# Weight tiles 32 bytes longer: the high and low parts of split weights start at other addresses

## The chip, the cores and the metric

The kernel runs on one core of a Trainium2 chip. The metric is the device time of one execution in microseconds. The engines named here are TensorE (PE; its weight loads are listed apart as PEld), VectorE (DVE), ScalarE (ACT), GpSimd (POOL) and SyncE (SP, which issues DMAs).

## The reference

One encoder layer on 512 tokens with 1,024 features, in float32. `x` passes three residual blocks, each behind an RMS norm with a shift and scale computed from a conditioning vector `c`:

```
x += 1/2 * g1 * SwiGLU_1(mod(RMSNorm(x)))
x += g2 * W_out( sig(gA) * W_A(WindowGQA+sink) + sig(gB) * W_B(DiffAttn) )
x += 1/2 * g3 * SwiGLU_2(mod(RMSNorm(x)))
```

The two SwiGLU blocks have an inner width of 2,816; `w_mod` (1,024 x 9,216) gives the nine modulation vectors. Between the blocks lie a windowed attention with 8 heads and a differential attention with 4 heads.

## The kernel before

All activations are kept feature-major: a tile holds 128 features and up to 512 tokens. To keep float32 accuracy on a faster matmul type, each operand is split into a high part (the value rounded to that type) and a low part (the rest), and a product is made of three matmuls: high weight by high activation, high weight by low activation, low weight by high activation. `mm3` (lines 153 to 156) does this with 512 or 256 tokens a matmul. In the second feed-forward block a Strassen-like scheme of seven products is used instead, and its helper `two` (lines 1098 to 1100) issues the same three matmuls with 256 tokens. In both, the weights are the stationary operand, which TensorE loads ahead of each matmul, and the activations the moving one. In `project` (lines 656 to 658) it is the other way round: activations are stationary and the weight tiles move through.

A weight block of 128 x 1,024 comes by DMA into a `raw` tile. `split_from` (lines 159 and 160) then writes the high part into a `hi` tile on ScalarE and the low part into a `lo` tile on VectorE. Four places allocate such a pair: `load_split` (first feed-forward, mixing, gates), `first_split` (the first eight blocks), `load_main` (projections and gates; there the low part is made by ScalarE and a DMA that adds), and `Unit.prepare` (second feed-forward). `hi` and `lo` have five buffers each, used in turn; the k-th pair of a stage has the same buffer number in both. Some weights go elsewhere: three gate blocks are split into `u4` tiles (`load_split(..., spare=True)`), and one block of the second feed-forward into a `b8` tile.

The order of the matmuls on TensorE is fixed by the program: written out by hand at the boundaries of the blocks, and by a list of items in the second feed-forward block. Weights are asked for some items ahead.

All tiles lie in one pool. It gives every kind of tile one stretch of each partition's memory, in order of first use, its buffers one behind the other, each size rounded up to 32 bytes. From the sizes in the kernel before, the starts in a partition are:

| kind | buffers x bytes | first start | start counted by 128 | by 512 |
|---|---|---|---|---|
| `u4` (gate weights, some activations) | 6 x 4,096 | 6,048 | 32 | 416 |
| `x` (residual) | 8 x 2,048 | 31,040 | 64 | 320 |
| `ka` | 1 x 4,096 | 47,712 | 96 | 96 |
| `b8` (split activations) | 12 x 8,192 | 51,808 | 96 | 96 |
| `f2` (scratch) | 8 x 2,048 | 150,112 | 96 | 96 |
| `raw` | 4 x 4,096 | 166,496 | 96 | 96 |
| `hi` | 5 x 4,096 | 182,880 | 96 | 96 |
| `lo` | 5 x 4,096 | 203,360 | 96 | 96 |

Inside a tile, weights begin at multiples of 512 bytes and activations at multiples of 1,024 (512 or 256 tokens), so every such operand of `ka`, `b8`, `hi` and `lo` begins at 96 by 512, and every one of `u4` at 416. [...]

Of the kernel before, what the change touches and what calls it, by code (L numbers as in the profile page):

```python
# [12 lines left out]
F32R = mybir.dt.float32r  # L13
# [5 lines left out]
P = 128  # L19
# [78 lines left out]
RAW, HILO, LO, F2 = 4, 5, 5, 8  # L98
# [16 lines left out]
def layer(ctx: ExitStack, tc: tile.TileContext, a: dict):  # L115
# [6 lines left out]
    def name(tag):  # L122
        count[0] += 1
        return f"{tag}_{count[0]}"

    def sbuf(tag, shape, dt, bufs):
        return sb.tile(shape, dt, name=name(tag), tag=tag, bufs=bufs)
# [4 lines left out]
    def f2():  # L132
        return sbuf("f2", [P, T], F32, F2)

    def b8(dt=F32R):
        return sbuf("b8", [P, 4, T], dt, 12)

    def u4(dt=F32R):
        return sbuf("u4", [P, 2, T], dt, 6)
# [4 lines left out]
    def bank(tag):  # L144
        return psum.tile([P, T], F32, name=name(tag), tag=tag, bufs={"acc": 3, "op": 1, "sc": 3, "tp": 1}[tag])
# [12 lines left out]
    def split_from(hi, lo, src):  # L158
        S.copy(hi, src)  # L159
        V.tensor_tensor(lo, src, f(hi), ALU.subtract)  # L160

    def load_split(src, n=1024, spare=False):
        raw = sbuf("raw", [P, 1024], F32, RAW)
        if spare:
            hi, lo = (u4().rearrange("p a b -> p (a b)") for _ in range(2))
        else:
            hi = sbuf("hi", [P, 1024], F32R, HILO)
            lo = sbuf("lo", [P, 1024], F32R, LO)
        nc.sync.dma_start(raw[:, 0:n], src)
        split_from(hi[:, 0:n], lo[:, 0:n], raw[:, 0:n])  # L170
        return hi, lo
# [22 lines left out]
    def mod_load(v, c):  # L194
        w = u4(F32).rearrange("p a b -> p (a b)")
        nc.sync.dma_start(w, a["w_mod"][v * NC + c])
        return w

    def mod_col(v, c, w=None, on_pool=False):
        if w is None:  # L200
            w = mod_load(v, c)
        t = modv[v][:, c : c + 1]
        if on_pool:
            S.activation(w, w, AF.Identity, accum_out=t)
        else:
            V.tensor_tensor_reduce(  # L206
                out=w, in0=w, in1=cact, scale=1.0, scalar=0.0, op0=ALU.mult, op1=ALU.add, accum_out=t
            )
        i = v * NC + c
        b = par[:, BMOD + i : BMOD + i + 1]  # L210
        if v in (SC1, SC2, SC3):
            n = {SC1: NORM1, SC2: NORM2, SC3: NORM3}[v]
            V.tensor_scalar(t, t, b, 1.0, ALU.add, ALU.add)
            V.tensor_tensor(t, t, par[:, n + c : n + c + 1], ALU.mult)
        elif v in (SH1, SH2, SH3):
            V.tensor_tensor(t, t, b, ALU.add)
        else:

            V.tensor_scalar(t, t, b, -0.5 if v == G3 and c % 4 < 2 else 0.5, ALU.add, ALU.mult)
# [62 lines left out]
    def hidden(rb, c, sc, sh, hi, lo, r=FULL[0]):  # L282

        t = f2()[:, r]
        s = modv[sh][:, c : c + 1]
        V.scalar_tensor_tensor(t, x[c][:, r], modv[sc][:, c : c + 1], rb, ALU.mult, ALU.mult)
        S.activation(hi[:, r], t, AF.Identity, bias=s)
        yield
        V.scalar_tensor_tensor(lo[:, r], t, s, f(hi[:, r]), ALU.add, ALU.subtract)
        yield  # L290
# [75 lines left out]
    def pair_banks():  # L366
        return (bank("acc"), bank("sc"))

    def ffn(w_in, w_out, g, hh, hl, begin, p, side, after_x, norm, loaded=None):
# [17 lines left out]
        for hf in range(2):  # L387
            while p < (hf + 1) * NH:
                u = loaded or [load_split(w_in[p, k]) for k in range(2)]
                loaded = None  # L390
                out = pair_banks()
                for k in range(NC):
                    ffn_pair_mm(u, k, out, hh, hl)
                finish(p, out)
                side(SIDE_IN)
                p += 1
# [34 lines left out]
    with tc.manual_schedule(engines={mybir.EngineType.DVE, mybir.EngineType.Activation, mybir.EngineType.PE}):  # L431
        cb = [bank("sc") for i in range(2)]
        for i in range(2):
            PE.matmul(cb[i], ones[0:1, :], crow[:, i * T : (i + 1) * T], start=True, stop=True)
        n1 = Norm()
        for c in range(NC):
            sq = f2()
            S.activation(sq, x[c], AF.Square)
            if c:
                V.tensor_tensor(sq, sq, before, ALU.add)  # L440
            before = sq
        n1.sums(sq, FULL[0], True, True)
        for i in range(2):
            S.activation(cact[:, i * T : (i + 1) * T], cb[i], AF.Silu)
        w1 = {}

        def first_loads(k):
            w1[k] = [mod_load(v, k) for v in ((SH1, SC1) if k else (SC1, SH1))]
            raw = sbuf("raw", [P, 1024], F32, RAW)
            nc.sync.dma_start(raw[:, 0:768], a["w1s"][k])  # L450
            w1[k].append(raw)
            if k:
                G.tensor_tensor(w1[k][0], w1[k][0], cact, ALU.mult)
                mod_col(SC1, k, w1[k][1])

        def first_split(k):
            hi = sbuf("hi", [P, 1024], F32R, HILO)
            lo = sbuf("lo", [P, 1024], F32R, LO)
            split_from(hi[:, 0:768], lo[:, 0:768], w1[k][2][:, 0:768])
            w1[k] = hi, lo  # L460

        first_loads(0)
        mod_col(SC1, 0, w1[0][0])
        rb1 = n1.spread(n1.diagonal(n1.rstd(FULL[0])))
        mod_col(SH1, 0, w1[0][1])
        first_split(0)
        out1 = [b for _ in range(3) for b in pair_banks()]
        for k in range(NC):
            h1 = hidden(rb1, k, SC1, SH1, hh[k], hl[k])
            next(h1)  # L470
            if k == 0:
                next(h1)
                first_loads(1)
            else:
                if k + 1 < NC:
                    first_loads(k + 1)
                next(h1)
            wh, wl = w1[k]
            for w, h in ((wh, hh[k]), (wl, hh[k]), (wh, hl[k])):
                for i, out in enumerate(out1):  # L480
                    last = k == NC - 1 and h is hl[k]
                    PE.matmul(out, w[:, i * P : (i + 1) * P], h, start=k == 0 and w is wh and h is hh[k], stop=last)
            if k + 1 < NC:
                mod_col(SH1, k + 1, w1[k + 1][0], on_pool=True)
                first_split(k + 1)
# [109 lines left out]
    def load_main(src):  # L595

        raw = sbuf("raw", [P, 1024], F32, RAW)
        nc.sync.dma_start(raw, src)
        hi = sbuf("hi", [P, 1024], F32R, HILO)
        lo = sbuf("lo", [P, 1024], F32R, LO)  # L600
        S.copy(hi, raw)
        S.activation(lo, raw, AF.Identity, scale=-1.0)
        G.dma_start(lo, src, accum_op=ALU.add)
        return hi, lo
# [12 lines left out]
    def first_gates(r):  # L617
# [13 lines left out]
    vb_w = boundary(  # L631
        last1, G1, n2, SC2, SH2, hh, hl, first_gates,
        lambda: [(load_split, load_main)[j // 2](a["w_vb"][j]) for j in range(4)],
        TO_MIX,
    )
# [28 lines left out]
    def gates(more=lambda: True):  # L664
        while gate_next[0] < 16 and more():
            j = gate_next[0]
            gate_next[0] += 1
            wh, wl = load_main(a["w_gate"][j])
            out = bank("acc")
            for k in range(NC):  # L670
                o = k * P
                mm3(out, wh[:, o : o + P], wl[:, o : o + P], hh[k], hl[k], k == 0, k == NC - 1)
                yield MM3
            gate_end(j, out)
# [427 lines left out]
    class Unit:  # L1102
# [25 lines left out]
        def prepare(self, q):  # L1128

            if q in self.ready:  # L1130
                return
            self.ask(q)
            n = self.depth * 2 * P
            if q in self.apart:
                both = b8().rearrange("p a b -> p (a b)")
                hi, lo = both[:, 0:n], both[:, 1024 : 1024 + n]
            else:
                hi = sbuf("hi", [P, 1024], F32R, HILO)[:, 0:n]
                lo = sbuf("lo", [P, 1024], F32R, LO)[:, 0:n]
            t = self.at[q]  # L1140
            split_from(hi, lo, t)
            self.ready[q] = hi, lo
            if q in self.more:
                s, src = self.more[q]
                G.dma_start(t, self.srcs[src], accum_op=ALU.add)
                self.at[s] = t
# [406 lines left out]
```

## Time and profile before

| | us |
|---|---|
| median of 3 runs | 1116.93 |
| lowest, highest | 1116.50, 1118.64 |
| the profiled execution | 1117.23 |
| its span, first to last instruction | 1115.4 |

| engine | busy us | share of span |
|---|---|---|
| TensorE, matmuls | 1086.0 | 97% |
| TensorE, weight loads | 950.5 | 85% |
| VectorE | 739.6 | 66% |
| ScalarE | 536.0 | 48% |
| GpSimd | 147.4 | 13% |

The views used below: the busy time of each engine in stretches of the span (the number behind x counts the instructions that begin there); the list of who waited for whom; groups of instructions by line with their shapes kept apart (count, then busy time and mean ns of one, then the idle time before them); and the instructions in order of time (start, length, engine, line, output <- inputs). Names of tiles are shortened there: `b` is `b8`, `u` is `u4`, `sc`, `acc`, `op` and `tp` are accumulators. Matmuls overlap, since one begins while the one ahead still drains, so the step from start to start, not the length, is what a matmul costs in a row of them.

### The profile page before, as it was taken

How to read it: one execution, taken by the hardware profiler on the slowest of the kernel's cores; microseconds unless marked ns; L12 is line 12 of the kernel's file. 1: busy time of each engine (PE TensorE's matmuls, PEld its weight loads, DVE VectorE, ACT ScalarE, POOL GpSimd, SP SyncE). 2: the span in 40 equal slices, each digit the busy share in tenths (PEclk: the TensorE clock that was granted, in tenths of full speed). 3: DMA queues.
4: the chain of work that ended last, by engine and by line, in shares of the span. 5: the costliest groups of instructions: out<-in, count | busy, mean ns of one | idle time of the engine just before them, and what ended most of it. 6: DMA issues, size and time to landing. Idle time of an engine off the chain costs nothing.

```text
span 1115.4 us, 16981 instructions
## 1 busy us (share of the span) xinstructions
PE 1086.0 (97%) x6540; PEld 950.5 (85%) x6540; DVE 739.6 (66%) x1441; ACT 536.0 (48%) x895; POOL 147.4 (13%) x152
## 2 busy tenths in 40 slices
PE   4899999999999999999999999999999999999998
PEld 2688888888888998876788877979999999999998
DVE  6998456765733450567642678855888777776767
ACT  3453221223223274567765655534766545654553
POOL 3300000000000011430113300101121111111210
PEclk9999999999999999999999999999999999999999
DMA  8797446766434439874468831862488999799874
GB/s 304 239 353 249 137 153 218 249 242 224 156 87 127 161 115 271 189 171 95 105 158 199 228 103 34 308 187 58 95 200 202 222 231 195 182 224 212 188 145 118
DMA packets 63570, 204.54 MB, mean 183 GB/s; under 512 B 7553, under 2 KB 9729, under 8 KB 63490
## 3 DMA queue, kind: packets, MB, share of 16 engines
q1 hardware_dynamic: 45792, 144.73, 37.6%
q0 software_dynamic: 15392, 54.53, 27.1%
q10 hardware_dynamic: 2306, 4.20, 1.0%
q8 instruction: 51, 0.84, 0.3%
q14 instruction: 29, 0.24, 0.1%
HBM read 194.52 MB, written 8.91 MB: 182 GB/s over the span
## 4 chain that ended last, share of the span: by engine, by line
PE 78%; issue 9%; DVE 5%; DMA 3%; ACT 2%; POOL 1%; SPq 0%; DVEq 0%; POOLq 0%; ACTq 0%
PE sc L154 9%; PE sc L156 9%; PE sc L155 9%; PE acc L154 7%; PE acc L155 6%; PE acc L156 6%; PE sc L1098 3%; PE sc L1100 3%; PE sc L1099 3%; PE acc L1099 3%; PE acc L1100 3%; PE acc L1098 3%; PE acc L656 2%; PE acc L657 2%; PE acc L658 2%
## 5 line engine op out<-in xcount | busy, mean ns | idle before, releaser
L159 ACT CAST hi<-raw 128x1024 fp32r<-128x1024 f32 (+2 forms) x160 | 155.3, 975 | 218.5 <-PE sc L155 130.9
L160 DVE TENSOR_TENSOR lo<-raw,hi 128x1024 fp32r<-128x1024 f32 (+2 forms) x160 | 179.9, 1129 | 60.6 <-ACT hi L159 58.4
L154 PE MATMUL sc<-b,hi 128*128 128x512 f32 (+1 forms) x430 | 159.9, 372 | 0.4 <-ACT b L159 0.4
L155 PE MATMUL sc<-b,hi 128*128 128x512 f32 (+1 forms) x430 | 159.3, 371 | 0.0
L156 PE MATMUL sc<-b,lo 128*128 128x512 f32 (+1 forms) x430 | 159.2, 370 | 0.0
L154 PE MATMUL acc<-b,hi 128*128 128x512 f32 (+1 forms) x352 | 134.1, 381 | 0.0
L155 PE MATMUL acc<-b,hi 128*128 128x512 f32 (+1 forms) x352 | 130.8, 372 | 0.0
L156 PE MATMUL acc<-b,lo 128*128 128x512 f32 (+1 forms) x352 | 130.7, 371 | 0.0
L1098 PE MATMUL acc<-b,hi 128*128 128x256 f32 x374 | 106.2, 284 | 0.1
L1099 PE MATMUL acc<-b,hi 128*128 128x256 f32 x374 | 105.9, 283 | 0.1
L1100 PE MATMUL acc<-b,lo 128*128 128x256 f32 x374 | 105.9, 283 | 0.0
L1100 PE MATMUL sc<-b,lo 128*128 128x256 f32 x358 | 101.4, 283 | 0.0
L1098 PE MATMUL sc<-b,hi 128*128 128x256 f32 x358 | 101.3, 283 | 0.0
L1099 PE MATMUL sc<-b,hi 128*128 128x256 f32 x358 | 101.3, 283 | 0.0
L154 PEld LDWEIGHTS sc<-b,hi 128*128 128x128 f32 x430 | 81.0, 188 | 14.7 <-ACT b L159 0.9
L155 PEld LDWEIGHTS sc<-b,hi 128*128 128x128 f32 x430 | 81.0, 188 | 14.2 <-DVE b L160 0.3
L156 PEld LDWEIGHTS sc<-b,lo 128*128 128x128 f32 x430 | 81.0, 188 | 13.7
L206 DVE CUSTOM_DVE_ANT_0 u<-u,ka 128x1024 f32<-128x1024 f32 x65 | 82.5, 1281 | 12.9 <-DMA u<-w_mod 12.8
L159 ACT CAST hi<-u 128x1024 fp32r<-128x1024 f32 (+1 forms) x51 | 52.2, 1024 | 69.1 <-PE acc L1099 14.1
L160 DVE TENSOR_TENSOR lo<-u,hi 128x1024 fp32r<-128x1024 f32 (+1 forms) x51 | 60.8, 1192 | 28.8 <-ACT hi L159 28.4
L154 PEld LDWEIGHTS acc<-b,hi 128*128 128x128 f32 x352 | 66.4, 189 | 13.7 <-issue 3.5
L156 PEld LDWEIGHTS acc<-b,lo 128*128 128x128 f32 x352 | 66.3, 188 | 11.3
(339 smaller groups left out, 2461.1 us busy)
## 6 DMA issues: line engine op xcount, KB each, us to landing
u<-w_mod SPq DMA_DIRECT2D x72, 512.0 KB, 5.3
raw<-w1i SPq DMA_DIRECT2D x38, 512.0 KB, 4.3
u<-w2i POOLq DMA_DIRECT2D x31, 512.0 KB, 6.1
raw<-w2i SPq DMA_DIRECT2D x31, 512.0 KB, 4.4
raw<-w_gate SPq DMA_DIRECT2D x16, 512.0 KB, 5.1
lo<-w_gate POOLq DMA_DIRECT2D x13, 512.0 KB, 7.3
u<-w2i SPq DMA_DIRECT2D x13, 512.0 KB, 6.9
raw<-w1o SPq DMA_DIRECT2D x16, 384.0 KB, 3.1
```

The lines of the kernel that those rows point to most:

```text
L154: PE.matmul(out, wh, xh, start=first, stop=False)
L155: PE.matmul(out, wh, xl, start=False, stop=False)
L156: PE.matmul(out, wl, xh, start=False, stop=last)
L159: S.copy(hi, src)
L160: V.tensor_tensor(lo, src, f(hi), ALU.subtract)
L206: V.tensor_tensor_reduce(out=w, in0=w, in1=cact, scale=1.0, scalar=0.0, op0=ALU.mult, op1=ALU.add, accum_out=t)
L656: PE.matmul(out[t][:, 0:n], hh[k][:, ht], wh[:, o : o + n], start=k == 0, stop=False)
L657: PE.matmul(out[t][:, 0:n], hh[k][:, ht], wl[:, o : o + n], start=False, stop=False)
L658: PE.matmul(out[t][:, 0:n], hl[k][:, ht], wh[:, o : o + n], start=False, stop=k == NC - 1)
L1098: PE.matmul(out, wh[:, s], xh, start=first and j == 0, stop=False, skip_group_check=True)
L1099: PE.matmul(out, wh[:, s], xl, start=False, stop=False, skip_group_check=True)
L1100: PE.matmul(out, wl[:, s], xh, start=False, stop=last and j == 1, skip_group_check=True)
```

## The change

The tiles `hi` and `lo` are declared with 1,032 in place of 1,024 columns, in all four places, and their first 1,024 columns are used as before. [...] `lo` begins 160 bytes further than before, and the tables behind it 320 bytes. No instruction, wait, transfer or order is added or taken away.

```diff
@@ load_split
-            hi = sbuf("hi", [P, 1024], F32R, HILO)
-            lo = sbuf("lo", [P, 1024], F32R, LO)
+            hi = sbuf("hi", [P, 1032], F32R, HILO)[:, 0:1024]
+            lo = sbuf("lo", [P, 1032], F32R, LO)[:, 0:1024]
@@ first_split
-            hi = sbuf("hi", [P, 1024], F32R, HILO)
-            lo = sbuf("lo", [P, 1024], F32R, LO)
+            hi = sbuf("hi", [P, 1032], F32R, HILO)[:, 0:1024]
+            lo = sbuf("lo", [P, 1032], F32R, LO)[:, 0:1024]
@@ load_main
-        hi = sbuf("hi", [P, 1024], F32R, HILO)
-        lo = sbuf("lo", [P, 1024], F32R, LO)
+        hi = sbuf("hi", [P, 1032], F32R, HILO)[:, 0:1024]
+        lo = sbuf("lo", [P, 1032], F32R, LO)[:, 0:1024]
@@ Unit.prepare
-                hi = sbuf("hi", [P, 1024], F32R, HILO)[:, 0:n]
-                lo = sbuf("lo", [P, 1024], F32R, LO)[:, 0:n]
+                hi = sbuf("hi", [P, 1032], F32R, HILO)[:, 0:n]
+                lo = sbuf("lo", [P, 1032], F32R, LO)[:, 0:n]
```

## The prediction

> **What bounds the kernel now.** I read the page's head and first part, then the busy time by stage, then TensorE's waits, and last, in order of time, the single matmuls, since the change moves addresses and nothing else. The page's first lines:
>
> ```profile
> span 1115.4 us, 16981 instructions
> PE 1086.0 (97%) x6540; PEld 950.5 (85%) x6540; DVE 739.6 (66%) x1441; ACT 536.0 (48%) x895; POOL 147.4 (13%) x152
> ```
>
> TensorE is busy 97% of the span. The sums below are made against this execution's own time, 1117.23 us (span 1115.4 and 1.8 around it); the median of the runs is 1116.93, so they differ by 0.03%. Three stretches of 56 us, with busy time and (x instructions) of PE, PEld, DVE, ACT and POOL, then the granted clock, the DMA share and GB/s:
>
> ```profile
> 56.00:112.00 56.00, 56.00 (x248) 46.16 (x247) 50.55 (x95) 23.14 (x32) 0.00 (x0) 1.00 0.83 300
> 840.00:896.00 56.00, 56.00 (x469) 56.00 (x469) 43.97 (x68) 32.70 (x52) 9.60 (x11) 1.00 0.88 212
> 896.00:952.00 56.00, 56.00 (x469) 56.00 (x469) 41.71 (x61) 30.05 (x43) 9.62 (x11) 1.00 0.93 215
> ```
>
> In the first feed-forward stage (56 to 112 us) TensorE takes 248 matmuls of 512 columns, 226 ns each; in the second (840 to 952 us) 469 of 256 columns, 119.4 ns each, and there the weight loads (PEld) fill all 56.00 us too. The clock is 1.00 in all three. TensorE's waits on a split are small; the longest in the list of waits (us in total, times, longest):
>
> ```profile
> PE acc L1100 <- DVE b L160: 0.8, 1, 0.8
> ```
>
> So TensorE's own step from matmul to matmul sets the time, and a weight tile's address can matter only through that step. Does it? The single matmuls (start, length, line) where the stationary operand goes over from a `hi`/`lo` buffer to a `u4` tile, while the moving operand stays in `b8`:
>
> ```profile
> 392.00 0.28 PE L154 MATMUL sc<-b,hi 128*128 128x256 f32 x1
> ...
> 392.96 0.28 PE L156 MATMUL sc<-b,lo 128*128 128x256 f32 x1
> 393.08 0.28 PE L154 MATMUL acc<-b,u 128*128 128x256 f32 x1
> 393.19 0.28 PE L155 MATMUL acc<-b,u 128*128 128x256 f32 x1
> ...
> 395.08 0.28 PE L156 MATMUL acc<-b,u 128*128 128x256 f32 x1
> ...
> 396.33 0.28 PE L156 MATMUL acc<-b,u 128*128 128x256 f32 x1
> ...
> 398.03 0.28 PE L156 MATMUL acc<-b,u 128*128 128x256 f32 x1
> ```
>
> From 392.00 to 393.08 there are nine steps with weights in `hi`/`lo`: 120.0 ns each. From 393.08 to 395.08 there are seventeen with weights in `u4`: 117.6 ns. After an interruption by eight short matmuls the same tiles go on at a third speed: fifteen steps from 396.33 to 398.03, 113.3 ns. The form, the clock and the moving tiles are the same. What differs between the first two is the start: `hi`, `lo` and `b8` begin at the same place in any 512 bytes, `u4` 64 bytes away from them by 128 (320 by 512). The same is seen where the moving operand goes to `u4` for six matmuls and the weights stay in `hi`/`lo`:
>
> ```profile
> 884.09 0.28 PE L1098 MATMUL acc<-u,hi 128*128 128x256 f32 x1
> ...
> 884.80 0.29 PE L1098 MATMUL op<-b,hi 128*128 128x256 f32 x1
> 884.93 0.28 PE L1099 MATMUL op<-b,hi 128*128 128x256 f32 x1
> ...
> 885.28 0.28 PE L1099 MATMUL op<-b,hi 128*128 128x256 f32 x1
> ```
>
> Six steps take 0.71 us, where 117.6 ns each would make 0.706 and 120.0 would make 0.72; then four steps back on `b8` take 0.48, the first of them 0.13. So a step of 256 columns depends on where the two operands begin relative to each other, and equal starts, the state of nearly all of this kernel, are the slow one of the two offsets seen.
>
> [...]
>
> **The change part by part.** (1) *New starts of the weights.* With 4,128 bytes a buffer, the five `hi` buffers begin 0, 32, 64, 96, 128 bytes further, and `lo`, behind them, 160 to 288 further. Counted by 128, against the moving `b8` tiles: `hi` 0, 32, 64, 96, 0; `lo` 32, 64, 96, 0, 32. Of three loads (hi, hi, lo) that makes (2 x 3/5 + 4/5) / 3 = 2/3 with a start that differs from the moving one. How many matmuls that is:
>
> ```profile
> L1098 PE MATMUL acc<-b,hi 128*128 128x256 f32 x374 | 106.2, 284 | 0.1
> L1098 PE MATMUL sc<-b,hi 128*128 128x256 f32 x358 | 101.3, 283 | 0.0
> L1098 PE MATMUL tp<-b,hi 128*128 128x256 f32 x66 | 18.7, 283 | 0.0
> L1098 PE MATMUL op<-b,hi 128*128 128x256 f32 x58 | 16.4, 283 | 0.0
> L154 PE MATMUL sc<-b,hi 128*128 128x256 f32 x76 | 22.0, 290 | 0.0
> L154 PE MATMUL acc<-b,hi 128*128 128x256 f32 x64 | 18.2, 284 | 0.0
> L154 PE MATMUL sc<-b,hi 128*128 128x512 f32 x354 | 137.8, 389 | 0.4 <-ACT b L159 0.4
> L154 PE MATMUL acc<-b,hi 128*128 128x512 f32 x288 | 115.9, 402 | 0.0
> L656 PE MATMUL acc<-hi,b 128*128 128x512 f32 x96 | 37.9, 395 | 0.0
> L656 PE MATMUL sc<-hi,b 128*128 128x512 f32 x32 | 12.7, 396 | 0.0
> ```
>
> Each row is one of three lines of a triple. 256 columns: 374 + 358 + 66 + 58 + 76 + 64 = 996 triples, 2,988 matmuls. Two thirds of them, 1,992, at 117.6 in place of 120.0 ns: 1,992 x 2.4 = 4.8 us less. Offsets of 32 and 96 bytes stand in no row of before, and I bound them by the nearest: 113.3 ns (gain 6.7 each, 13.3 us in all) and the 0.13 us step of 884.80, 10 ns worse. I take 117.6, the one value that both offsets seen (weights 64 away, moving operand 64 away) give in steady state.
>
> (2) *Changes of offset inside a triple.* `hi` and `lo` of a pair will differ by 32 bytes, so each triple goes over and back. The rows have two prices. When the weights change from `hi`/`lo` to `u4` (392.96 to 393.19) the steps are 0.12 and 0.11: nothing. When the moving operand goes there and back, the ten steps from 884.09 to 885.28 lose 0.004 going in and 0.003 coming out against pure speeds, 7 ns. 996 triples x 7 ns = 7.0 us at most. I take nothing, since here the weights change and not the moving tile, and keep the 7.0 for the range.
>
> (3) *Matmuls of 512 columns.* (354 + 288) x 3 = 1,926 with `hi`/`lo` as weights and (96 + 32) x 3 = 384 with them as the moving operand, 2,310 in all. Their step in both cases of start, the second with the moving operand in `u4`:
>
> ```profile
> 99.86 0.39 PE L154 MATMUL acc<-b,hi 128*128 128x512 f32 x1
> ...
> 102.35 0.39 PE L156 MATMUL sc<-b,lo 128*128 128x512 f32 x1
> 682.54 0.39 PE L155 MATMUL op<-u,b 128*128 128x512 f32 x1
> 682.76 0.40 PE L156 MATMUL op<-u,b 128*128 128x512 f32 x1
> ```
>
> Eleven steps in 2.49 us are 226 ns, and the one between `u4` starts is 0.22 to the row's hundredth. A weight load is hidden in so long a matmul (46.16 us of PEld in 56). I take no change, bounded by the prices of (1) and (2): 2/3 x 2,310 x 2.4 = 3.7 us less, 770 triples x 7 ns = 5.4 us more.
>
> (4) *Splits, DMAs, other tiles.* VectorE and ScalarE read and write these buffers; VectorE's two groups:
>
> ```profile
> L160 DVE TENSOR_TENSOR lo<-raw,hi 128x1024 fp32r<-128x1024 f32 x112 | 136.3, 1222 | 30.8 <-ACT hi L159 29.2
> L160 DVE TENSOR_TENSOR lo<-u,hi 128x1024 fp32r<-128x1024 f32 x45 | 55.1, 1224 | 24.2 <-ACT hi L159 23.8
> ```
>
> With the source in `raw` (start equal to `hi`) and in `u4` (64 away) it takes 1222 and 1224 ns: nothing, and both engines have idle time in the rows by stage (44 and 33 us busy of 56) that would hide some. The number of instructions, waits and DMAs stays. The tiles allocated behind `lo` move by 320 bytes, 64 by 128: tables of the rotary embedding and small columns, read by VectorE and ScalarE: nothing, hidden in the same idle time.
>
> (5) *Cover.* A 256-column stage that is 2% shorter asks 2% more of its transfers: the highest DMA share rises from 0.93 to 0.95, which still fits. At 5.6% (113.3 ns throughout) it would be 0.98, and late weights would take some back.
>
> Sum: -4.8 + 0 + 0 + 0: 1117.2 - 4.8 = 1112.4 us.
>
> **The rivals.** *Faster still:* the shifted weights fall into the 113.3 ns state. For it: the trace has that state with unchanged addresses, after an interruption, so it is stable once entered. Against: it is seen in this one passage of 2 us, and 117.6 in both places. 1,992 x 6.7 = 13.3 us: 1103.9.
>
> *Slower, changes of offset cost:* the mechanism of (2) at its full price, in the 256-column triples, with a gain only at the offset that was seen, 64 bytes (`hi` and `lo` one buffer in five each: 598 matmuls, 1.4 us). 7.0 - 1.4 = 5.6 us more: 1122.8. For it: the 0.13 us step at 884.80, and that every triple would change over. Against: the change of weights at 393.08 was free. With all gains of (1) kept, it decides from 4.8 us / 996 = 4.8 ns a triple on.
>
> [...]
>
> **How the numbers follow.** Likeliest case 0.32 (own range 1109 to 1115), faster still 0.17, slower 0.33, no change 0.18. A measurement of this kernel tells about 0.2%, 2.2 us, from no change, so faster 0.49, same 0.18, slower 0.33. The range takes in most of the fast rival (1103.9, a little less with some of the 512-column gain) and the slow rival with part of (3)'s loss: 1102 to 1125.
>
> **What would show it.** In the rows by stage, 840 to 952 us: x469 in 56 us becomes about 475 if (1) holds (two thirds at 117.6), 487 in the 113.3 state, below 469 if the changes over cost. In order of time: steps of 0.117 to 0.118 inside a triple for four of five pairs, and 0.13 after a change of buffer only if (2) is wrong. The stage from 56 to 112 us keeps x248 if (3) holds. The mean of 1222 ns stays if (4) holds. Wrong it would be most easily by the offsets of 32 and 96 bytes, of which before says nothing.

## The result and the profile after

The changed kernel is slower: 1122.87 us median against 1117.57 us for the kernel before in the same session, a ratio of 1.0053 with a 95% interval of 1.0038 to 1.0068. The forecast was 1112.4, faster. The page's first lines, and the same three stretches by stage, with one more (busy time and count of PE, PEld, DVE, ACT, POOL, then clock, DMA share, GB/s):

```profile
span 1120.6 us, 16981 instructions
PE 1092.2 (97%) x6540; PEld 946.1 (84%) x6540; DVE 738.8 (66%) x1441; ACT 536.1 (48%) x895; POOL 149.4 (13%) x152
```

```profile
56.00:112.00 56.00, 56.00 (x243) 45.22 (x242) 49.40 (x95) 22.85 (x31) 0.00 (x0) 1.00 0.81 296
840.00:896.00 56.00, 55.89 (x472) 55.68 (x472) 44.97 (x71) 33.39 (x53) 10.44 (x12) 1.00 0.89 209
896.00:952.00 56.00, 56.00 (x475) 55.90 (x474) 42.22 (x61) 28.80 (x41) 10.47 (x12) 1.00 0.93 223
952.00:1008.00 56.00, 56.00 (x476) 56.00 (x475) 43.41 (x65) 33.86 (x52) 8.66 (x10) 1.00 0.90 205
```

The last of these stretches in the kernel before:

```profile
952.00:1008.00 56.00, 56.00 (x469) 56.00 (x469) 42.14 (x59) 32.06 (x50) 10.43 (x12) 1.00 0.88 199
```

Two things happened, of opposite sign. The 256-column stage went from x469 to x472, x475 and x476, near the 475 that step (1) had given. The 512-column stage went from x248 to x243. The number behind x counts all instructions that run in a stretch, not only those that begin there, so it takes in the matmuls already under way at its start, and 56 us / x comes out 0.5 to 2 ns shorter than a step. The steps themselves, from the start of one matmul to the start of the next, are in these stretches 226.7 ns before and 232.4 after with 512 columns, and 119.9 and 118.5 with 256. (All such means in this part are over the matmuls of triples, 56 to 112 us for 512 columns and 840 to 1,008 us for 256.)

Set side by side, the n-th matmul of either trace shows where the time runs away. Lag of the changed kernel against the one before, both counted from their first matmul:

| n-th matmul | 400 | 800 | 1200 | 1600 | 2000 | 3000 | 4000 | 5000 | 6000 |
|---|---|---|---|---|---|---|---|---|---|
| its time in the kernel before, us | 116 | 207 | 298 | 381 | 447 | 639 | 803 | 923 | 1043 |
| lag, us | 1.8 | 3.9 | 6.2 | 7.8 | 8.5 | 9.8 | 9.0 | 7.8 | 6.3 |

The first feed-forward block loses 1.1 us per 200 matmuls of 512 columns; the attention in the middle, where TensorE waits for other engines part of the time (188.72 us busy of the 192.00 from 450.30 to 642.30 us of the span in the kernel before), adds 1.3 us from the 2,000th to the 3,000th; the second feed-forward block gives back some 0.3 us per 200 matmuls of 256 columns. At the last matmul the lag is 5.8 us, so 4.0 of the 9.8 are won back; the span grew by 5.2 us. The steps in the first block, one by one (start, length):

```profile
99.77 0.40 PE L154 MATMUL sc<-b,hi 128*128 128x512 f32 x1
100.01 0.39 PE L155 MATMUL sc<-b,hi 128*128 128x512 f32 x1
100.24 0.40 PE L156 MATMUL sc<-b,lo 128*128 128x512 f32 x1
...
102.34 0.40 PE L156 MATMUL acc<-b,lo 128*128 128x512 f32 x1
```

Eleven steps in 2.57 us are 233.6 ns, where the kernel before took eleven in 2.49. No wait and no gap has appeared in this stretch: TensorE is busy 56.00 of 56.00 us. The splits kept their length, as the group by line shows:

```profile
L160 DVE TENSOR_TENSOR lo<-raw,hi 128x1024 fp32r<-128x1024 f32 x112 | 136.4, 1222 | 29.6 <-ACT hi L159 27.3
L160 DVE TENSOR_TENSOR lo<-u,hi 128x1024 fp32r<-128x1024 f32 x45 | 55.1, 1224 | 26.3 <-ACT hi L159 25.9
```

### The profile page after: what moved, and what is told of

Same layout as the page of the kernel before. It is cut to its first block, busy times and chain, and to the rows that moved or that the text cites. A ratio compares the mean times of both kernels' runs of the same rounds, so it can differ in the third digit from the quotient of the medians.

```text
span 1120.6 us, 16981 instructions
## 1 busy us (share of the span) xinstructions
PE 1092.2 (97%) x6540; PEld 946.1 (84%) x6540; DVE 738.8 (66%) x1441; ACT 536.1 (48%) x895; POOL 149.4 (13%) x152
## 4 chain that ended last, share of the span: by engine, by line
PE 77%; issue 10%; DVE 5%; DMA 3%; ACT 2%; POOL 1%; SPq 0%; POOLq 0%; DVEq 0%; ACTq 0%
PE sc L154 9%; PE sc L156 9%; PE sc L155 9%; PE acc L154 7%; PE acc L155 7%; PE acc L156 7%; PE acc L658 2%; PE acc L656 2%; PE acc L1098 2%; PE acc L1100 2%; PE acc L657 2%; PE acc L1099 2%; PE sc L1098 2%; PE sc L1100 2%; PE sc L1099 2%
## 5 line engine op out<-in xcount | busy, mean ns | idle before, releaser
L155 PEld LDWEIGHTS sc<-b,hi 128*128 128x128 f32 x430 | 80.8, 188 | 15.6
```

The lines of the kernel that those rows point to most:

```text
L155: PE.matmul(out, wh, xl, start=False, stop=False)
```

## The experiments

Two theories came from this. CHANGE: a 512-column matmul is longer when successive weight loads begin at different offsets, as they do in every triple of the changed kernel. OFFSET: it is longer when the load begins an odd multiple of 32 bytes from the moving tile. Neither lived; a third, RELATIVE, came out of the first four runs. All times are medians, with the kernel before run on the same chip beside them.

### All weight buffers 32 bytes further

```diff
@@ first_split, ahead of hi
+            if k == 0:
+                V.memset(keep([P, 8], "pad"), 0.0)
```

> Buffers of 4,096 bytes as in the kernel before, and one tile of 32 bytes ahead of hi, so that every hi and lo buffer begins 32 bytes further than before, all at the same offset to b8. Theory CHANGE (the 512-column matmuls of the changed kernel lose because successive weight loads begin at different offsets, whatever these are): no change of offset is left, so 512 columns go back to x248 in 56 to 112 us; 256 columns at 117.6 to 120 ns; time 1110 to 1118. Theory OFFSET (a load that begins an odd multiple of 32 bytes from the moving tile costs, whatever was loaded ahead of it): every load is odd where the changed kernel had 0.47 of them, so 512 columns lose about 12 ns each, x235 in 56 to 112 us, and the time is some 1135.

Measured: 1125.68 us, ratio 1.0073 (1.0058 to 1.0088). With no change of offset left at all, the 512-column stage is slower still, x241:

```profile
56.00:112.00 56.00, 56.00 (x241) 45.02 (x240) 49.16 (x93) 23.66 (x32) 0.00 (x0) 1.00 0.82 300
896.00:952.00 56.00, 56.00 (x476) 56.00 (x476) 41.87 (x59) 29.77 (x40) 8.68 (x10) 1.00 0.95 225
```

CHANGE falls. OFFSET had the sign, but a far greater loss (x235, 1135).

### All weight buffers 64 bytes further

The same edit with a tile of 16 columns.

> As the kernel before with one tile of 64 bytes ahead of hi: every hi and lo buffer begins 64 bytes further, the offset that u4 weights had. Both CHANGE and OFFSET: 512 columns stay at x248 in 56 us; 256 columns go at 117.6 ns, x476 in 896 to 952 us; 2,988 x 2.4 = 7.2 us less, some 1110. If the 113.3 ns state is entered: some 1098.

Measured: 1114.47 us, ratio 0.9978 (0.9967 to 0.9989), a little faster than the kernel before.

```profile
56.00:112.00 56.00, 56.00 (x242) 45.17 (x242) 49.19 (x95) 22.87 (x31) 0.00 (x0) 1.00 0.80 295
840.00:896.00 56.00, 56.00 (x479) 56.00 (x478) 45.62 (x73) 33.98 (x53) 10.44 (x12) 1.00 0.91 217
896.00:952.00 56.00, 56.00 (x493) 56.00 (x492) 43.78 (x64) 30.51 (x44) 10.46 (x12) 1.00 0.93 228
952.00:1008.00 56.00, 56.00 (x496) 56.00 (x495) 43.51 (x62) 34.34 (x52) 10.42 (x12) 1.00 0.90 213
```

x242 with 512 columns: 64 bytes are an even multiple, and the loss is there all the same. OFFSET falls too. With 256 columns the state of 113.3 ns is not a rarity any more: from start to start the three stretches have 117.5, 114.1 and 113.4 ns. One kernel thus holds a loss in the first block and a gain in the second, from the same shift.

### Only the low parts 32 bytes further

```diff
@@ first_split, between hi and lo
+            if k == 0:
+                V.memset(keep([P, 8], "gap"), 0.0)
```

> As the kernel before with a tile of 32 bytes between hi and lo: hi begins as before, every lo 32 bytes further, so there is no stepping from buffer to buffer, but each triple of loads (hi, hi, lo) changes its offset twice. CHANGE: 512 columns as in the changed kernel, x243 in 56 to 112 us, time 1118 to 1125. OFFSET: only one load in three is odd, in place of 0.47: 512 columns lose 3.9 in place of 5.5 ns, x244, time some 1120. A theory that it is the stepping from buffer to buffer that costs: x248 and 1113 to 1118.

Measured: 1125.16 us, ratio 1.0071 (1.0056 to 1.0086).

```profile
56.00:112.00 56.00, 56.00 (x242) 45.01 (x241) 49.25 (x94) 23.83 (x32) 0.00 (x0) 1.00 0.82 299
840.00:896.00 56.00, 56.00 (x476) 56.00 (x475) 45.09 (x71) 34.06 (x55) 10.45 (x12) 1.00 0.90 214
952.00:1008.00 56.00, 56.00 (x475) 56.00 (x474) 44.42 (x67) 34.29 (x54) 10.31 (x12) 1.00 0.86 198
```

One unequal load in three brings the whole loss. So it is not a sum over the loads: counted over the steps of this trace, the matmul during which `lo` is loaded takes 238 ns, the next 229, the third 232, some 233 on the mean, near the 232 to 234 that all other shifts have. With 256 columns one unequal load in three brings the whole gain too: x476 and x475, 118.3 ns, where all loads unequal by 32 bytes have 118.2. (The stretch between them has x470, with TensorE idle for 0.51 us of it.)

### Pairs with equal offsets

```diff
+            hi = sbuf("hi", [P, 1032], F32R, HILO)[:, 0:1024]
+            if k == 0:
+                V.memset(keep([P, 24], "gap"), 0.0)
+            lo = sbuf("lo", [P, 1032], F32R, LO)[:, 0:1024]
```

> 1,032 columns as in the changed kernel and a tile of 96 bytes between hi and lo, so that the hi and lo of a pair begin at the same offset (0, 32, 64, 96, 0): offsets change only from one pair to the next, not inside a triple. CHANGE: 512 columns nearly back, x247 to x248 in 56 to 112 us; 256 columns at 117.6 ns for three pairs of five, time 1110 to 1116. OFFSET: 0.4 of the loads odd, 512 columns lose 4.7 ns, x243, time 1119 to 1123.

Measured: 1121.94 us, ratio 1.0043 (1.0027 to 1.006).

```profile
56.00:112.00 56.00, 56.00 (x243) 45.29 (x242) 49.47 (x95) 22.75 (x31) 0.00 (x0) 1.00 0.80 295
```

The changes inside the triples are gone and the loss is not, which speaks against CHANGE a second time. Taken by pair over the whole trace, the 512-column steps on a pair at equal starts are 228 ns, and those on the other four pairs 233 to 234, within one kernel.

The four runs leave RELATIVE: what counts is where the weights begin against the moving tile. Equal starts, which the kernel before had nearly throughout, are the fast case with 512 columns (227 ns against some 233) and the slow one with 256 columns (120 against 113 to 118).

### Is "equal" counted by 128 bytes?

Buffers of 4,224 bytes; to make room for them the DMA scratch space is halved:

```diff
+            hi = sbuf("hi", [P, 1056], F32R, HILO)[:, 0:1024]
+            lo = sbuf("lo", [P, 1056], F32R, LO)[:, 0:1024]
...
+    nc = bacc.Bacc("TRN2", ..., dynamic_dma_scratch_size=2048)
```

> hi and lo with 1,056 columns, of which the first 1,024 are used: buffers of 4,224 bytes, so that every start is the same by 128 as in the kernel before (equal to b8) while by 256 it alternates. To make room the DMA scratch space is 2,048 in place of 4,096 bytes. Theory RELATIVE (what counts is the start of the weights against that of the moving tile by 128 bytes: equal starts are the fast case for 512 columns, 226.7 ns against 233, and the slow one for 256 columns, 120 against 113 to 118): nothing changes, x248 in 56 to 112 us, x469 in 896 to 952 us, 1117. If starts count by 256 or more: x242 to x245 and x472 or more, 1115 to 1122.

Measured: 1124.14 us, ratio 1.0072 (1.0057 to 1.0087).

```profile
56.00:112.00 56.00, 56.00 (x243) 45.35 (x242) 49.46 (x94) 23.26 (x32) 0.00 (x0) 1.00 0.81 300
896.00:952.00 56.00, 56.00 (x475) 56.00 (x474) 42.37 (x61) 28.86 (x41) 10.53 (x12) 1.00 0.90 222
```

So 128 bytes are not "equal". (The smaller scratch space is not the cause: the run with equal starts by 256 bytes, below, has it too.) Counted over the steps of this trace, 512-column matmuls between two loads of a `hi` buffer with equal starts by 256 take 227.5 ns, and those where either load is 128 away 232 to 235.

Two more runs had been laid out on the wrong period, before this one was measured:

> As two0, but the weights of the 256-column matmuls of the second feed-forward block (Unit.prepare) and of the product with w_ya are put into columns 16 to 1,039, 64 bytes further, and those of the 512-column matmuls stay at equal starts. RELATIVE: both stages in their fast case, x248 in 56 to 112 us as before and x493 to x496 from 896 to 1,008 us as with all buffers 64 bytes further: 1117.1 - 15.6 = 1101.5. The 15.6 is worked out from that run: its time is 2.7 us less, and its 512-column steps cost 2,310 x 5.6 ns = 12.9 us more. CHANGE (successive loads at different offsets) would give the same, since there is no change within a stage. If the time of a step depends on something else than the start, 1117.

> As two64 with the roles exchanged: weights of 512-column matmuls 64 bytes further, those of 256-column matmuls at equal starts. RELATIVE: both stages in their slow case, x242 in 56 to 112 us and x469 in 896 to 952 us, 1117.1 + 12.9 = 1130. CHANGE: x248 and x469, 1117.

Their edits are those of two runs with 1,088 columns below ("Each stage in its fast case" and "The roles exchanged"), with 1,056 columns. They gave 1115.14 us (ratio 0.9998, 0.9974 to 1.0022; single executions from 1112.0 to 1126.4) and 1121.51 us (1.0044, 1.0029 to 1.0058), both with x243 in the first block. The second block followed its offset: x490 and x496 in the two stretches from 896 us with the 64 bytes, x475 and x473 without.

> As the kernel before with a tile of 96 bytes ahead of hi, every hi and lo 96 bytes further. RELATIVE: 512 columns slow as with every unequal start, x241 to x243 in 56 to 112 us; 256 columns at 118 ns as with 32 bytes (x476) or at 113 as with 64 bytes (x493). Time 1125 if like 32 bytes, 1114 if like 64 bytes.

The edit is that of "All weight buffers 32 bytes further", with a tile of 24 columns. Measured: 1126.18 us (1.0092, 1.0072 to 1.0113), x241 and x476: 96 bytes are like 32 in both stages.

### Equal starts by 256 bytes

```diff
-        return sbuf("sm", [P, 8], F32, 24)[:, 0:n]
+        return sbuf("sm", [P, 8], F32, 22)[:, 0:n]
...
+            hi = sbuf("hi", [P, 1088], F32R, HILO)[:, 0:1024]
+            lo = sbuf("lo", [P, 1088], F32R, LO)[:, 0:1024]
```

> hi and lo with 1,088 columns, the first 1,024 used: buffers of 4,352 bytes, so that every start is equal to b8 by 256, and by 512 it alternates. To make room the DMA scratch space is 2,048 in place of 4,096 bytes and there are 22 in place of 24 small tiles of 32 bytes, so that everything lies 2,112 bytes lower. Theory RELATIVE-256 (only the start against the moving tile by 256 bytes counts; by 128, as theory RELATIVE had it, was too short): x248 in 56 to 112 us, x469 in 896 to 952 us, 1117. If starts count by 512 or more, or the place in memory itself counts: x243, 1122.

The scratch space is 2,048 as in the run with 1,056 columns. Measured: 1117.00 us, ratio 1.0000 (0.9988 to 1.0011).

```profile
56.00:112.00 56.00, 56.00 (x248) 46.21 (x248) 50.52 (x98) 22.86 (x31) 0.00 (x0) 1.00 0.82 301
896.00:952.00 56.00, 56.00 (x469) 56.00 (x469) 42.02 (x61) 29.66 (x43) 9.63 (x11) 1.00 0.94 215
```

Nearly every tile lies 2,112 bytes lower, the buffers of `hi` and `lo` have another length, their starts by 512 bytes alternate, and both counts are those of the kernel before. 256 bytes apart is equal and 128 is not, so starts count by 256. Counted so, 2,112 bytes are 64, and 64 bytes between weights and moving tile had made x242; moving both by 64 changes nothing, so by this run it is the one start against the other that counts and not the place in memory.

### Each stage in its fast case

On top of the run before, 64 bytes for the weights of the 256-column matmuls (the other two places keep columns 0 to 1,023):

```diff
-    def load_split(src, n=1024, spare=False):
+    def load_split(src, n=1024, spare=False, o=0):
...
+            hi = sbuf("hi", [P, 1088], F32R, HILO)[:, o : o + 1024]
+            lo = sbuf("lo", [P, 1088], F32R, LO)[:, o : o + 1024]
@@ main, the product with w_ya
-            yield from branch(a["w_ya"], 0, *wa["o"], then_b, load_split, r)
+            yield from branch(a["w_ya"], 0, *wa["o"], then_b, lambda w: load_split(w, o=16), r)
@@ Unit.prepare
+                hi = sbuf("hi", [P, 1088], F32R, HILO)[:, 16:16 + n]
+                lo = sbuf("lo", [P, 1088], F32R, LO)[:, 16:16 + n]
```

> As eq256, but the weights of the 256-column matmuls of the second feed-forward block and of the product with w_ya lie 64 bytes further, in columns 16 to 1,039. RELATIVE-256: x248 in 56 to 112 us and x490 to x496 from 896 to 1,008 us, 1117.1 - 15.6 = 1101.5. If starts count by 512 or more: 512 columns at x243 as in the run with 1,056 columns, 1112 to 1115.

Measured: 1106.56 us against 1117.37, ratio 0.9905 (0.989 to 0.9919): faster than both kernels.

```profile
56.00:112.00 56.00, 56.00 (x248) 46.18 (x247) 50.56 (x96) 23.09 (x32) 0.00 (x0) 1.00 0.83 300
840.00:896.00 56.00, 56.00 (x480) 55.93 (x479) 44.73 (x70) 31.91 (x49) 10.44 (x12) 1.00 0.91 212
896.00:952.00 56.00, 55.09 (x484) 54.89 (x483) 42.41 (x63) 31.65 (x47) 9.64 (x11) 1.00 0.92 218
952.00:1008.00 56.00, 56.00 (x493) 55.83 (x493) 42.53 (x61) 32.70 (x48) 10.45 (x12) 1.00 0.94 222
```

The first block keeps x248 and the second gains, but the 15.6 us that I expected came to 10.8. Most of that was a wrong sum: I had charged the run with 64 bytes 12.9 us for its 512-column matmuls, and set side by side with the kernel before it had lost 8.8 us by the 2,000th matmul and 9.6 by the 3,000th; between them lies the attention, where TensorE is idle for 3.28 us of 192.00 in the kernel before. That its waits took up what my sum had too much is an estimate; no run shows it. From the 3,000th matmul on, the gain is nearly that run's, 12.7 us here and 13.0 there. What is left is a lag of 1.7 us that arises between the 2,000th and the 3,000th matmul; the run with equal starts has 1.6 there and the run with 128 bytes below none, so it does not follow the offsets, and its cause is open. In the stretch from 896 us TensorE is idle for 0.91 us, and not for late weights but for one copy by ScalarE (the list of waits in this stretch):

```profile
PE sc L1098 <- ACT f L1165: 0.9, 1, 0.9
```

### The roles exchanged

The same kernel with columns 16 to 1,039 for the weights of the 512-column matmuls and 0 to 1,023 for the others.

> As best with the roles exchanged: weights of the 512-column matmuls 64 bytes further, those of the 256-column matmuls at equal starts. RELATIVE-256: both stages in their slow case, x242 in 56 to 112 us, x469 in 896 to 952 us, 1117.1 + 12.9 = 1130. If starts count by 512 or more: 256 columns at x473 or more, 1121 to 1126.

Measured: 1126.39 us, ratio 1.0084 (1.0069 to 1.0099). Both stages are in their slow case:

```profile
56.00:112.00 56.00, 56.00 (x242) 45.09 (x241) 49.25 (x92) 22.39 (x31) 0.00 (x0) 1.00 0.81 297
896.00:952.00 56.00, 56.00 (x470) 56.00 (x469) 42.22 (x59) 28.34 (x39) 8.72 (x10) 1.00 0.95 224
```

It is 9 us over equal starts and not 13, by the same error of my sum. Between these last two kernels, which do the same work with the same buffers, lie 20 us.

### 128 bytes for the 256-column stage

The kernel above with columns 32 to 1,055 in place of 16 to 1,039.

> As best, but the weights of the 256-column matmuls lie 128 in place of 64 bytes from equal starts. RELATIVE-256: 128 is unequal, so these stages gain against x469 in 896 to 952 us; by the run with 1,056 columns, where starts alternated by 128, x473 to x475 (118.5 ns), so 2,988 x 1.4 = 4 us less than equal starts, 1113. If 64 is no better than any unequal start: as best, 1106.5. If 128 counts as equal for 256 columns: x469, 1117.

Measured: 1113.49 us, ratio 0.9973 (0.9962 to 0.9985), with x248 in the first block and

```profile
896.00:952.00 56.00, 56.00 (x474) 56.00 (x473) 42.08 (x62) 30.38 (x45) 9.54 (x11) 1.00 0.90 217
```

128 bytes give 118.7 ns from start to start. Of the offsets tried for a whole stage, only 64 bytes lead into the 113 ns state.

## Why the prediction was wrong

*Step (1), the new starts, was right in its sign and near in size for 256 columns, in part by luck.* x475 had been given and x472, x475 and x476 were measured; 4.8 us forecast, 4.0 won back after the 3,000th matmul. The unknown offsets of 32 and 96 bytes, which I named as the weak point, turned out near the 117.6 ns that I took: 118.2 ns each from start to start. But the sum counted starts by 128 bytes, by which 2/3 of the loads differ from the moving tile, where they count by 256, by which 4/5 do. And it let the gain go with that share, where 32 bytes on the low parts alone, one load in three, brought the whole gain.

*Step (2), the changes of offset inside a triple, cost next to nothing with 256 columns,* as I took it: the run with pairs of equal offsets has 118.1 ns from start to start, the changed kernel 118.5.

*Step (3) is the one that failed.* I put the 512-column matmuls at no change, with 5.4 us as the worst case; the lag grew to 9.8 us by the 3,000th matmul, and 2,226 of these first 3,000 are matmuls of 512 columns with `hi` and `lo`. The bound was made of the 7 ns a triple of step (2), where a step grew by 5.7 ns, 17 ns a triple. And the row of before that I took for it misled: of the matmuls with the moving operand in `u4` I showed one step of 0.22 us. These are others of the same group, in the kernel before:

```profile
654.85 0.40 PE L156 MATMUL op<-u,b 128*128 128x512 f32 x1
655.08 0.39 PE L154 MATMUL op<-u,b 128*128 128x512 f32 x1
655.32 0.39 PE L155 MATMUL op<-u,b 128*128 128x512 f32 x1
655.55 0.39 PE L156 MATMUL op<-u,b 128*128 128x512 f32 x1
```

Three steps in 0.70 us, 233 ns each: unequal starts, and the price that the changed kernel then paid. The 36 back-to-back steps of that group average 231.7 ns; I took one of the shortest for the rule. The argument that a weight load is hidden in so long a matmul was also wrong as a reason: the loads still fill only 45.22 us of 56, and the step is longer all the same. How a load and a matmul meet, no run shows. The counts were a little low as well: 144 matmuls of line 482 are missing from the 2,310, and some 100 triples (moving operand in `u4` or `ka`, or `hi` and `lo` moving with 256 columns) from the 996; neither turns a sign.

*Steps (4) and (5) held.* 1222 and 1224 ns stayed, and with 64 bytes throughout the DMA share was 0.93 at x493 and 0.90 at x496 with TensorE busy 56.00 of 56.00 us, so the transfers kept up.

*The rivals.* The slower rival gave 1122.8, and 1122.87 came, but that is luck, for the mechanism was another: it had put its cost into the triples of 256 columns, which gained. The faster rival's state exists, and with 64 bytes throughout it is entered (113.4 ns from 952 us on), though not with a step of 32 bytes from buffer to buffer (118.5). No change at all, to which I gave 0.18, did not come either, and the runs speak against it in both stages: with nothing changed but the start of the weights, a step takes 227 or 233 ns with 512 columns, and 113 to 120 with 256.

## What to carry to other kernels

Where TensorE is the bound and weight loads run beside matmuls, look at the start of the stationary tile against the moving one as one looks at a wait: here it moved the time by 20 us of 1,117 without an instruction being changed. The good offset differed with the number of columns, and one layout for both stages traded one for the other: 1114.47 us with 64 bytes throughout, 1106.56 with 64 bytes for the 256-column stage alone. Take the offset from the steps of each stage. And when one row has to stand for a case that the trace barely shows, take the mean of its group, not the row that suits the sum.

## What the runs showed of the hardware

Step of a matmul of this type from start to start, by the start of the weights against the moving tile, both counted by 256 bytes (means over the triples from 56 to 112 us and from 840 to 1,008 us; for 64 bytes the least and the greatest of that run's three stretches):

| offset, bytes | 512 columns, ns | 256 columns, ns |
|---|---|---|
| 0 | 226.7 | 119.9 |
| 32 | 233.4 | 118.2 |
| 64 | 233.3 | 113.4 to 117.5 |
| 96 | 234.2 | 118.2 |
| 0 and 128 mixed | 231.9 | 118.7 |
| 128 | | 118.7 |

I had not expected that the same shift speeds one shape up and slows the other down, nor that one unequal load in three costs as much as three (some 233 ns against 233.4 with 512 columns). Left open: by what mechanism the starts act, why the two shapes differ in sign, why with 64 bytes the step sits at 117 ns for some time and then at 113, and what offsets below 32 bytes or, for a whole stage, between 128 and 256 do, which was not tried.
